# Layer 1's folded product moved into four PSUM banks, with sums and differences sharing a bank, and gate banks copied out under a raised priority

## The chip, the core and the metric

The kernel runs on one core of a Trainium2 chip. The metric is device time in microseconds (us) from start to end of one execution. TensorE (PE) multiplies and transposes, VectorE (DVE) and ScalarE (ACT) do elementwise work and read PSUM, GpSimd (POOL) and SyncE (SP) mostly issue DMAs. PSUM has eight banks of 512 fp32 columns; this kernel keeps them in two pools of four, named `pa` and `pm`.

## The reference

Two layers of a post-norm encoder over 512 tokens of width 2048, all in fp32. Per layer:

```python
mod = silu(c) @ w_ada[l] + b_ada[l];  shift, scale, gate = split(mod, 3)
h = layernorm(x) * (1 + scale) + shift
u_f, z_f, cq, ckv, k_r, z_a = split(h @ w_in[l], [1024, 2048, 2560, 2816, 2880])
# group A: 8 groups of 128 channels, 2-D FFT over tokens and channels, real part, a 128x128 map
y_f = einsum("sgc,gcd->sgd", real(fftn(u_f, axes=(s, c), norm="ortho")), w_fmix[l]) * silu(z_f)
# group B: latent attention, 8 heads, rotary key shared
y_a = attention(rmsnorm(cq) @ w_q_b, rmsnorm(ckv) @ w_kv_b, k_r) * silu(z_a)
x = layernorm(ALPHA * x + gate * (concat(y_f, y_a) @ w_out[l]), ln_g, ln_b)
```

## The kernel before, in words

Every fp32 product is made of three fp32r products: each operand is split into a high and a low part (`split`, lines 145 to 147: ACT casts the high part, line 146, then DVE subtracts, line 147), and `mm3` (lines 149 to 152) issues high·high, high·low and low·high. A weight unit is loaded by SP into a raw buffer `wr` (three of them), split by ACT and DVE, and then used by PE. The fp32 weights thus pass through ACT and DVE on their way to PE.

Layer 1 works on folded tokens: `h` holds sums of tokens t and t+256 in columns 0 to 255 and their differences in columns 256 to 511. Its input products run in this order: gate group ZA0 (`first_group`), gate group ZF0 (`fm_group`), the constants of the Fourier part (`folded_constants`), the folded Fourier product (`u_pass`), gate group ZF1 with the Fourier work in between (`fm_group` with `runner(fb, FW)`), then the latents CQ and CKV, and gate group ZA1. A gate group fills four `pa` banks; `unfolded` (lines 841 to 849) copies each bank out with ACT (line 845), forms sum and difference on DVE (lines 846, 847), applies SiLU on ACT (line 848) and stores to DRAM by SP (line 849).

`folded_constants` multiplies six 128x512 plain-fp32 products (line 554) into six `pm` banks, one after another in the four that there are. Each of the first kind is read in halves by ACT (line 561) and DVE (line 562), each of the second kind in four quarters by ACT (line 420) and DVE (line 421). The left operands are built by DVE copies (lines 550, 552).

`u_pass` takes 16 weight units from `fold_unit` (lines 390 to 408), each 1024 columns wide: 520 columns that go with the token sums (0 to 519) and 504 that go with the differences (520 to 1023). For each unit and each of two token halves p it issues three products: 264 columns into a `pa` bank, 256 columns into a `pm` bank, 504 columns into another `pa` bank. So it uses four `pa` and two `pm` banks. Afterwards the banks are split into `ue`, `un` and `uo`, and the row of token 0 (`xacc`, summed up on DVE) is multiplied by ones (lines 785, 786).

The order of instructions on each engine is set by a list scheduler when the program is built; at run time each engine goes through its list in that order, and waits by semaphores. `tc.high_priority(offset=...)` raises what is inside it in that scheduler. A bank from a pool is given again when its readers are done.

Of the kernel before, what the change touches and what calls it, by code (L numbers as in the profile page):

```python
# [18 lines left out]
P = 128  # L19
S = 512  # L20
D = 2048
NT = S // P
NK = D // P
# [59 lines left out]
def trunk_kernel(ctx: ExitStack, tc: tile.TileContext, x, c, positions, w_ada, b_ada, w_in, q_norm,  # L83
# [15 lines left out]
    ROWS, LR = [0, 2, 1, 3], 600  # L99

    FW, UAH = 2, 6


    XE, RN0, PL, WL = 8, 2, 1, 2
    V, A, GP, PE, SP = nc.vector, nc.scalar, nc.gpsimd, nc.tensor, nc.sync
# [14 lines left out]
    def nm(s):  # L120
        uid[0] += 1
        return f"{s}{uid[0]}"

    def big(shape, dt=F32R):
        return bp.tile(shape, dt, tag="b", name=nm("b"))
# [4 lines left out]
    def t2(shape, dt=F32):  # L130
        return t2p.tile(shape, dt, tag="t2", name=nm("t2"))
# [4 lines left out]
    def pa():  # L136
        return psa.tile([P, 512], F32, tag="pa", name=nm("pa"))

    def pm():
        return psm.tile([P, 512], F32, tag="pm", name=nm("pm"))  # L140

    def f(ap):
        return ap.bitcast(F32)

    def split(hi, lo, src):
        A.copy(hi, src)  # L146
        V.tensor_tensor(lo, src, f(hi), op=ALU.subtract)  # L147

    def mm3(o, lh, ll, rh, rl, first, last):
        PE.matmul(o, lh, rh, start=first, stop=False)  # L150
        PE.matmul(o, lh, rl, start=False, stop=False)  # L151
        PE.matmul(o, ll, rh, start=False, stop=last)  # L152
# [13 lines left out]
    for tb in range(NT):  # L166
        t = [big([P, 1024], F32) for _ in range(2)]
# [283 lines left out]
    st = Stream(4, 2)  # L451
# [167 lines left out]
    h = [None] * NK  # L619
# [34 lines left out]
    for l in range(DEPTH):  # L654
# [91 lines left out]
            return u  # L746


        def u_pass():

            e, o, b = [pa(), pa()], [pa(), pa()], [pm(), pm()]
            for k in range(NK):
                wh, wl = st.next()
                for p in range(2):
                    es, os_ = slice(p * P, p * P + P), slice(256 + p * P, 256 + p * P + P)
                    for bank, ts, cs in ((e[p], es, slice(256, 520)), (b[p], es, slice(0, 256)),
                                         (o[p], os_, slice(520, 1024))):
                        mm3(bank[:, :cs.stop - cs.start], h[k][:, 0, ts], h[k][:, 1, ts], wh[:, cs], wl[:, cs],
                            k == 0, k == NK - 1)
            un = big([P, 2, 2, 2, P])  # L760
            GP.memset(f(un), 0.0)
            ue, uo = [], []
            for p in range(2):
                t = big([P, 2, 512])
                split(t[:, 0, 256:512], t[:, 1, 256:512], e[p][:, 0:256])
                split(un[:, 0, p, 0, 120:128], un[:, 0, p, 1, 120:128], e[p][:, 256:264])
                ue.append(t)
            for p in range(2):
                t = big([P, 2, 8, 64])
                split(t[:, 0, :, 1:64], t[:, 1, :, 1:64], o[p][:, :504].rearrange("p (g c) -> p g c", c=63))  # L770
                for a in range(2):
                    V.memset(f(t[:, a, :, 0]), 0.0)
                uo.append(t.rearrange("p a g c -> p a (g c)"))
            for p in range(2):
                split(ue[p][:, 0, 0:256], ue[p][:, 1, 0:256], b[p][:, 0:256])

            onesr = t2([P, P], F32R)
            V.memset(f(onesr), 1.0)
            xa = big([P, 1024])
            xl = big([P, 1024])  # L780
            split(xa[:, :520], xl[:, :520], xacc[0][:, :520])
            xr = big([1, 2, 512])
            for c0, c1 in ((0, 256), (256, 520)):
                ps = pm()
                PE.matmul(ps[:, :c1 - c0], onesr, xa[:, c0:c1], start=True, stop=False)
                PE.matmul(ps[:, :c1 - c0], onesr, xl[:, c0:c1], start=False, stop=True)
                split(xr[0:1, 0, c0:c0 + 256], xr[0:1, 1, c0:c0 + 256], ps[0:1, 0:256])
                if c1 == 520:
                    split(un[0:1, 1, 0, 0, 120:128], un[0:1, 1, 0, 1, 120:128], ps[0:1, 256:264])
            return ue, uo, un, xr  # L790

        def fourier_folded(u):
            ue, uo, un, xr = u

            def cosines(dst, kk, rr, n):
                ps = pm()
                for k in range(2):
                    mm3(ps[:, 0:258], kk[k][0], kk[k][1], dt[k][:, 0, 0:258], dt[k][:, 1, 0:258], k == 0, False)
                for a in range(2):
                    PE.matmul(ps[:, 0:258], rr[a], odd, start=False, stop=a == 1)  # L800
                split(dst[:, 0, 0:n], dst[:, 1, 0:n], ps[:, 0:n])

            an = big([P, 2, S])
            cosines(an, [(un[:, 0, k, 0], un[:, 0, k, 1]) for k in range(2)], [un[0:1, 1, 0, a] for a in range(2)], 258)
            yield
            for b in range(4):
                bs = slice(b * P, b * P + P)
                at = big([P, 2, S])
                cosines(at, [(ue[k][:, 0, bs], ue[k][:, 1, bs]) for k in range(2)], [xr[0:1, a, bs] for a in range(2)], 257)
                ps = pm()  # L810
                for k in range(2):
                    mm3(ps[:, 0:256], uo[k][:, 0, bs], uo[k][:, 1, bs], dt[k][:, 0, 256:512], dt[k][:, 1, 256:512],
                        k == 0, k == 1)
                split(at[:, 0, 257:512], at[:, 1, 257:512], ps[:, 1:256])
                yield
                yf.append(big([P, 2, S], F32))
                for i in range(2):
                    g = 2 * b + i
                    y = yf[-1][:, i]
                    gs = slice((g % 4) * P, (g % 4) * P + P)  # L820
                    c, s_, n = cw[0][g // 4], cw[1][g // 4], nq[g // 4]
                    pp, pq = pm(), pm()
                    mm3(pp[:, 0:258], c[:, 0, gs], c[:, 1, gs], at[:, 0, 0:258], at[:, 1, 0:258], True, False)
                    mm3(pp[:, 0:258], n[:, 0, gs], n[:, 1, gs], an[:, 0, 0:258], an[:, 1, 0:258], False, True)
                    mm3(pq[:, 0:256], s_[:, 0, gs], s_[:, 1, gs], at[:, 0, 256:512], at[:, 1, 256:512], True, True)
                    ev = t2([P, 258])
                    A.copy(ev, pp[:, 0:258])
                    V.tensor_tensor(y[:, 1:256], ev[:, 1:256], pq[:, 1:256], op=ALU.subtract)
                    V.tensor_tensor(y[:, 257:512], ev[:, 1:256], pq[:, 1:256], op=ALU.add)
                    V.tensor_copy(y[:, 0:257:256], ev[:, 0:257:256])  # L830
                    yield
# [8 lines left out]

        def unfolded(banks, dst):

            for j in range(4):
                t, z = t2([P, S]), t2([P, S])
                A.copy(t, banks[j])
                V.tensor_tensor(z[:, 0:256], t[:, 0:256], t[:, 256:512], op=ALU.add)
                V.tensor_tensor(z[:, 256:512], t[:, 0:256], t[:, 256:512], op=ALU.subtract)
                A.activation(z, z, AF.Silu, scale=0.5)
                SP.dma_start(szd[dst + j], z)

        def runner(gen, n=1):
            def run():
                for _ in range(n):
                    next(gen, None)
            return run
# [229 lines left out]
        if l == 0:  # L1085

            for step, (k0, nk) in enumerate(STEPS):
# [44 lines left out]
                def pas():  # L1132
                    return [pa() for _ in range(NT)]

                def pieces(gen, then=iter(())):
                    def run():
                        next(then, None)
                        for _ in range(2):
                            next(gen, None)
                    return run  # L1140
# [6 lines left out]
                ub = k_group(UB, pas(), pieces(fa, lq))  # L1147
# [3 lines left out]
                fb = fourier(1, folded(ub))  # L1151
# [14 lines left out]
        else:  # L1166
            unfolded(first_group(), 0)
            st.ahead(4, UAH)
            with tc.issue_after(hold[0]):
                banks = fm_group(ada=G0)  # L1170
            unfolded(banks, H)
            cw, nq, dt = folded_constants(1)
            st.ahead(4, 2)
            fb = fourier_folded(u_pass())
            unfolded(fm_group(runner(fb, FW)), H + 4)
            drain(fb)
            gt = gates()
# [17 lines left out]
        es, pts = {}, {}  # L1195
        for i in range(len(todo) + WL):
# [9 lines left out]
            if i < 4:  # L1206
                for k in range(2 * i, 2 * i + 2):
                    t = big([P, 2, S])
# [36 lines left out]
        for g in range(4):  # L1245
            gs = slice(g * 512, (g + 1) * 512)
# [3 lines left out]
            if g < 3:  # L1250
                banks = [pa() for _ in range(NT)]
                for k2 in range(8):
                    tm_half(banks, st.next(), y, k2 * 2, 512, k2 == 0, k2 == 7)
                    if g == 0:
                        tb, j = k2 // 2, k2 % 2
# [11 lines left out]
            else:  # L1267
# [4 lines left out]
                banks = [pa() for _ in range(NT)]  # L1272
# [7 lines left out]
                for tb in ROWS if l == 0 else range(NT):  # L1280
                    ts = slice(tb * P, (tb + 1) * P)
                    for k in range(KO * 2, NK):
                        wh, wl = ws[k // 2 - KO]
# [68 lines left out]
```

## Time and profile before

| | |
|---|---|
| median of 3 runs | 1406.38 us (1401.28 to 1406.9) |
| the profiled execution | 1404.26 us, span 1402.5 us |
| PE busy | 1344.3 us, 96% of the span |
| DVE, ACT, POOL busy | 72%, 41%, 4% |
| mean granted TensorE clock | 0.990 |

Times in the trace are us from the start of the span. The rows further down give start, duration, engine, line and operation; output and inputs follow as tile names without numbers, then the shape; a bracket at the end tells how long the engine sat idle before and what ended that. Matmuls are pipelined, so their durations overlap: the distance between starts is what one costs.

### The profile page before, as it was taken

To read this page: it belongs to the slowest core of one execution; us is meant where nothing else is said; L and a number is where in the kernel's file an instruction comes from. 1 tells how busy PE (TensorE), PEld (TensorE's weight loads), DVE (VectorE), ACT (ScalarE), POOL (GpSimd) and SP (SyncE) were. 2 spreads that over 40 slices of the span, in tenths; PEclk is the share of its full clock that TensorE was granted. 3 is DMA by queue.
4 is the path that set the end of the run, shared out by engine and by line. 5 is a ranking of instruction groups with operands and counts; after the bars stand their busy time and mean duration, and the time that the engine had idled before them with its cause. 6 is when DMAs were issued, how large, how long until landed. Compare 5 with 4: busy or idle time off the path is not lost. (4 is left out here: it accounts for less than half of the span.)

```text
span 1402.5 us, 18691 instructions
## 1 busy us (share of the span) xinstructions
PE 1344.3 (96%) x6949; PEld 1141.2 (81%) x6949; DVE 1015.6 (72%) x1670; ACT 579.6 (41%) x1052; POOL 55.5 (4%) x82
## 2 busy tenths in 40 slices
PE   4899999999999999999988999998999999999996
PEld 3688888787888888788877888887898888888885
DVE  7899999849978986658588748567655576642448
ACT  6722332224437776112167524323234677721210
POOL 1000000000000000000030001011000000000001
PEclk9999999999999999999998999999999999999998
DMA  9988898824764444968336435369444221263323
GB/s 288 299 293 300 271 349 286 306 76 122 211 206 140 157 128 161 317 199 283 105 145 203 161 96 166 105 205 367 152 119 121 74 67 54 80 236 105 91 60 120
DMA packets 134546, 253.24 MB, mean 181 GB/s; under 512 B 19308, under 2 KB 50168, under 8 KB 134456
## 3 DMA queue, kind: packets, MB, share of 16 engines
q1 hardware_dynamic: 127416, 228.73, 50.1%
q0 software_dynamic: 7040, 23.34, 4.9%
q8 instruction: 54, 0.88, 0.3%
q14 instruction: 36, 0.29, 0.1%
HBM read 237.32 MB, written 14.70 MB: 180 GB/s over the span
## 5 line engine op out<-in xcount | busy, mean ns | idle before, releaser
L150 PE MATMUL pa<-b,b 128*128 128x512 f32 (+4 forms) x1432 | 537.4, 377 | 11.6 <-ACT b L146 5.5
L151 PE MATMUL pa<-b,b 128*128 128x512 f32 (+4 forms) x1432 | 535.9, 375 | 4.3 <-DVE ln_v L187 4.3
L152 PE MATMUL pa<-b,b 128*128 128x512 f32 (+4 forms) x1432 | 534.5, 374 | 1.9 <-DVE b L147 1.9
L146 ACT CAST b<-wr 128x1024 fp32r<-128x1024 f32 (+3 forms) x184 | 180.0, 988 | 356.1 <-PE pa L152 181.1
L150 PEld LDWEIGHTS pa<-b,b 128*128 128x128 f32 x1432 | 271.2, 190 | 59.7 <-ACT b L146 9.2
L151 PEld LDWEIGHTS pa<-b,b 128*128 128x128 f32 x1432 | 272.1, 190 | 48.1 <-DVE ln_v L187 4.6
L152 PEld LDWEIGHTS pa<-b,b 128*128 128x128 f32 x1432 | 271.5, 190 | 48.2 <-DVE b L147 2.9
L147 DVE TENSOR_TENSOR b<-wr,b 128x1024 fp32r<-128x1024 f32 (+3 forms) x184 | 208.1, 1141 | 136.5 <-PE pa L151 84.7
L246 DVE SCALAR_TENSOR_TENSOR acc<-ada,cact,acc 128x1024 f32<-128x1024 f32 (+2 forms) x193 | 227.2, 1184 | 23.1 <-DMA ada<-in_w_ada_dram 21.2
L150 PE MATMUL pm<-b,b 128*128 128x512 f32 (+3 forms) x594 | 201.7, 341 | 1.2 <-ACT b L146 0.8
L151 PE MATMUL pm<-b,b 128*128 128x512 f32 (+3 forms) x594 | 197.2, 333 | 0.0
L152 PE MATMUL pm<-b,b 128*128 128x512 f32 (+3 forms) x594 | 197.0, 333 | 0.0
L150 PEld LDWEIGHTS pm<-b,b 128*128 128x128 f32 x594 | 111.7, 189 | 17.8 <-ACT b L146 2.7
L151 PEld LDWEIGHTS pm<-b,b 128*128 128x128 f32 x594 | 112.3, 189 | 10.5
L152 PEld LDWEIGHTS pm<-b,b 128*128 128x128 f32 x594 | 112.2, 189 | 10.4
L146 ACT CAST b<-pm 128x512 fp32r<-128x512 f32 (+4 forms) x110 | 54.9, 530 | 72.6 <-PE pm L800 17.8
L147 DVE TENSOR_TENSOR b<-pm,b 128x512 fp32r<-128x512 f32 (+4 forms) x110 | 64.1, 610 | 23.6 <-ACT b L146 23.0
L1120 DVE TENSOR_TENSOR b<-b,pm 128x512 f32<-128x512 f32 (+1 forms) x88 | 55.5, 656 | 4.5 <-PE pm L152 4.1
L146 ACT CAST b<-t 128x512 fp32r<-128x512 f32 (+1 forms) x73 | 35.9, 525 | 31.4 <-PE pm L151 9.5
L1039 DVE TENSOR_REDUCE mx<-pa 128x1 f32<-128x512 f32 x64 | 42.9, 684 | 5.3 <-PE pa L1037 4.7
L1044 ACT ACTIVATE t<-t,ssum 128x512 f32<-128x512 f32 x64 | 45.9, 735 | 1.2 <-DVE ssum L1043 1.2
L1042 ACT ACTIVATE t<-pa,mx 128x512 f32<-128x512 f32 x64 | 44.0, 693 | 4.6 <-DVE mx L1039 4.5
(186 smaller groups left out, 1120.7 us busy)
## 6 DMA issues: line engine op xcount, KB each, us to landing
wr<-in_w_in_dram SPq DMA_DIRECT2D x105, 512.0 KB, 4.6
ada<-in_w_ada_dram SPq DMA_DIRECT2D x96, 512.0 KB, 5.3
wr<-in_w_out_dram SPq DMA_DIRECT2D x64, 512.0 KB, 4.1
ada<-in_w_ada_dram SPq DMA_DIRECT2D x96, 256.0 KB, 4.9
ada<-in_w_ada_dram POOLq DMA_DIRECT2D x32, 512.0 KB, 5.4
b<-in_x_dram SPq DMA_DIRECT2D x16, 512.0 KB, 6.3
ada<-in_w_ada_dram SPq DMA_DIRECT2D x32, 192.0 KB, 5.3
wr<-in_w_q_b_dram SPq DMA_DIRECT2D x48, 128.0 KB, 3.0
```

Source lines behind the costliest of these rows:

```text
L146: A.copy(hi, src)
L147: V.tensor_tensor(lo, src, f(hi), op=ALU.subtract)
L150: PE.matmul(o, lh, rh, start=first, stop=False)
L151: PE.matmul(o, lh, rl, start=False, stop=False)
L152: PE.matmul(o, ll, rh, start=False, stop=last)
L246: V.scalar_tensor_tensor(out=a, in0=t[:, r - r0], scalar=cact[:, r:r + 1], in1=a, op0=ALU.mult, op1=ALU.add)
L1039: V.reduce_max(mx, ps, axis=AX.X, negate=True)
L1042: A.activation(e, ps, AF.Exp, bias=mx, accum_out=ssum)
L1044: A.activation(e, e, AF.Copy, scale=ssum)
L1120: V.tensor_tensor(s_[tb], s_[tb], banks[tb][:, :n], op=ALU.add)
```

## The change

Only layer 1 is touched. `u_pass` becomes `u_start`, `u_step` and `u_finish`. All of the folded product now lies in four `pm` banks, two for each token half p. Each bank holds 260 of the 520 sum columns in its columns 0 to 259 and 252 of the 504 difference columns in its columns 260 to 511, so that each unit and half has four products (260, 260, 252, 252 columns) in place of three. Only the first product in a bank has the start flag. The split after it reads each bank in two or three pieces. The columns of zeros in `uo` are set by POOL and no longer by DVE. `unfolded` copies all four banks first, under `tc.high_priority(offset=300)`, and needs four temporaries up front.

```diff
+    EV = 300
-        def u_pass():
-            e, o, b = [pa(), pa()], [pa(), pa()], [pm(), pm()]
-            for k in range(NK):
-                wh, wl = st.next()
-                for p in range(2):
-                    es, os_ = slice(p * P, p * P + P), slice(256 + p * P, 256 + p * P + P)
-                    for bank, ts, cs in ((e[p], es, slice(256, 520)), (b[p], es, slice(0, 256)),
-                                         (o[p], os_, slice(520, 1024))):
-                        mm3(bank[:, :cs.stop - cs.start], h[k][:, 0, ts], h[k][:, 1, ts], wh[:, cs], wl[:, cs],
-                            k == 0, k == NK - 1)
+        def u_start():
+            return [[pm(), pm()] for _ in range(2)]
+        def u_step(banks, k):
+            wh, wl = st.next()
+            hk = h[k]
+            for p in range(2):
+                for x in range(2):
+                    ts = slice(256 * x + p * P, 256 * x + p * P + P)
+                    n = 252 if x else 260
+                    for b in range(2):
+                        cs = slice(520 * x + b * n, 520 * x + b * n + n)
+                        mm3(banks[p][b][:, 260 * x:260 * x + n], hk[:, 0, ts], hk[:, 1, ts], wh[:, cs], wl[:, cs],
+                            k == 0 and x == 0, k == NK - 1 and x == 1)
+        def u_finish(banks):
...
+                a, b = banks[p]
                 t = big([P, 2, 512])
-                split(t[:, 0, 256:512], t[:, 1, 256:512], e[p][:, 0:256])
+                split(t[:, 0, 0:260], t[:, 1, 0:260], a[:, 0:260])
+                split(t[:, 0, 260:512], t[:, 1, 260:512], b[:, 0:252])
+                split(un[:, 0, p, 0, 120:128], un[:, 0, p, 1, 120:128], b[:, 252:260])
...
+                for i, ps in enumerate((a, b)):
+                    gs = slice(4 * i, 4 * i + 4)
+                    split(t[:, 0, gs, 1:64], t[:, 1, gs, 1:64], ps[:, 260:512].rearrange("p (g c) -> p g c", c=63))
+                for x in range(2):
+                    GP.memset(f(t[:, x, :, 0]), 0.0)
...
         def unfolded(banks, dst):
+            ts = [t2([P, S]) for _ in range(4)]
+            with tc.high_priority(offset=EV):
+                for j in range(4):
+                    A.copy(ts[j], banks[j])
             for j in range(4):
-                t, z = t2([P, S]), t2([P, S])
-                A.copy(t, banks[j])
+                t, z = ts[j], t2([P, S])
```

The order of instructions changes at a few places. Line numbers of the changed kernel are 2 higher up to `u_pass` and 10 to 16 higher behind it: 152 to 154 are `mm3`, 148 and 149 `split`, 556 the products of the constants, 423 their quarters on DVE, 856 the copies of `unfolded`. Numbers in names tell tiles apart.

Place 1 is the start of the folded product, where the constants are made. On PE before, four of the six products of the constants are followed by folded products into `pa` banks; the last two come in between:

```order
L554 MATMUL pm_7851<-b_7811,b_7848 128x512
L150 MATMUL pa_7889<-b_7552,b_6732 128x264
L151 MATMUL pa_7889<-b_7553,b_6732 128x264
L152 MATMUL pa_7889<-b_7552,b_6732 128x264
L150 MATMUL pa_7891<-b_7552,b_6732 128x504
L554 MATMUL pm_7862<-b_7811,b_7859 128x512
L554 MATMUL pm_7872<-b_7811,b_7870 128x512
```

On PE now, the six stand together and the folded product behind them; its fourth bank, `pm_7892`, is entered after two products of the second unit:

```order
L154 MATMUL pm_7891<-b_7552,b_6732 128x252
L152 MATMUL pm_7889<-b_7592,b_6735 128x260
L153 MATMUL pm_7889<-b_7593,b_6735 128x260
L152 MATMUL pm_7892<-b_7552,b_6732 128x260
L153 MATMUL pm_7892<-b_7553,b_6732 128x260
L154 MATMUL pm_7892<-b_7552,b_6732 128x260
```

What moved: before, the first product into a `pm` bank of the folded product stands behind 19 of its products into `pa` banks; now all of them go to `pm`, the pool that the constants use.

At the same place on DVE now, where `pm_7872` is the bank of the last constant (`fc_7874` its result), and `b_7993`, `wr_7941` belong to a weight unit:

```order
L400 TENSOR_TENSOR b_7993<-wr_7941 128x504
L423 SCALAR_TENSOR_TENSOR fc_7874<-pm_7872,ident,fc_7874 128x128
L410 SCALAR_TENSOR_TENSOR xacc_7560<-b_7993,orow,xacc_7560 128x520
L149 TENSOR_TENSOR b_7995<-b_7993,b_7994 128x1024
L423 SCALAR_TENSOR_TENSOR fc_7874<-pm_7872,ident,fc_7874 128x128
```

The last read of `pm_7872` stands behind the subtraction of a whole weight unit there, as it did before. Further up on DVE the copies that build left operands of the constants (line 550 before) now stand ahead of the sums and differences of all four gate banks:

```order
L552 COPY b_7848<-b_7809 128x64 x2
L552 COPY b_7859<-b_7809 128x64
L859 TENSOR_TENSOR t_7789<-t_7781 128x256
L860 TENSOR_TENSOR t_7789<-t_7781 128x256
L859 TENSOR_TENSOR t_7794<-t_7782 128x256
```

Before, the sums and differences of three banks came first:

```order
L552 COPY b_7835<-b_7809 128x128
L846 TENSOR_TENSOR t_7782<-t_7781 128x256
L847 TENSOR_TENSOR t_7782<-t_7781 128x256
L846 TENSOR_TENSOR t_7789<-t_7788 128x256
L847 TENSOR_TENSOR t_7789<-t_7788 128x256
L846 TENSOR_TENSOR t_7796<-t_7795 128x256
L847 TENSOR_TENSOR t_7796<-t_7795 128x256
L550 COPY b_7848<-b_7809 128x64 x2
L550 COPY b_7859<-b_7809 128x64 x2
```

Place 2 is the end of the folded product, on ACT. Before, the reads of the six banks alternate between banks; the cast of `xacc` comes after eight of them:

```order
L146 CAST b_8321<-pa_7889 128x256
L146 CAST b_8321<-pm_7893 128x256
L146 CAST b_8319<-pa_7889 128x8
L146 CAST b_8326<-pa_7890 128x256
L146 CAST b_8331<-pa_7891 128x8x63
L146 CAST b_8326<-pm_7894 128x256
L146 CAST b_8319<-pa_7890 128x8
L146 CAST b_8336<-pa_7892 128x8x63
L146 CAST b_8347<-xacc_7560 128x520
```

Now two or three reads of one bank follow each other; DVE has the same order:

```order
L148 CAST b_8415<-pm_7889 128x260
L148 CAST b_8422<-pm_7889 128x4x63
L148 CAST b_8415<-pm_7890 128x252
L148 CAST b_8413<-pm_7890 128x8
L148 CAST b_8422<-pm_7890 128x4x63
L148 CAST b_8429<-pm_7891 128x260
L148 CAST b_8436<-pm_7891 128x4x63
L148 CAST b_8445<-xacc_7560 128x520
```

On PE the product that takes the cast of `xacc` (line 785, now 795) stood six products behind the folded product, and stands three behind it now.

Place 3 is ACT after gate group ZF1, where `pa_8364` to `pa_8367` before (`pa_8462` to `pa_8465` now) are its banks and `wr_8872`, `wr_8905` before (`wr_8970`, `wr_9003` now) are weight units of CQ. Before:

```order
L845 COPY t_8836<-pa_8364 128x512
L845 COPY t_8843<-pa_8365 128x512
L848 ACTIVATE t_8837<-t_8837 128x512
L146 CAST b_8934<-wr_8872 128x1024
L848 ACTIVATE t_8844<-t_8844 128x512
L845 COPY t_8850<-pa_8366 128x512
L146 CAST b_8967<-wr_8905 128x1024
L845 COPY t_8857<-pa_8367 128x512
```

And now:

```order
L856 COPY t_8934<-pa_8462 128x512
L148 CAST b_9032<-wr_8970 128x1024
L856 COPY t_8935<-pa_8463 128x512
L856 COPY t_8936<-pa_8464 128x512
L148 CAST b_9065<-wr_9003 128x1024
L856 COPY t_8937<-pa_8465 128x512
```

The SiLUs moved behind the copies; the two weight casts stay among the copies, the first of them one copy earlier. After ZF0 and ZA1 the four copies now stand together; after ZA0 one weight cast stays before the fourth.

## Rows read from the trace of the kernel before

**Rows 1.** stretches: length, busy PE, PEld, DVE, ACT, POOL, granted clock, DMA, GB/s

```profile
840.00:891.00 51.00, 51.00 (x306) 43.95 (x305) 42.40 (x79) 24.36 (x60) 4.90 (x7) 1.00 0.55 160
891.00:949.00 58.00, 58.00 (x313) 49.32 (x312) 32.87 (x54) 15.38 (x30) 7.92 (x15) 1.00 0.51 161
949.00:963.00 14.00, 10.25 (x37) 7.24 (x36) 8.94 (x17) 6.90 (x11) 1.58 (x3) 0.84 1.04 405
```

**Rows 2.** groups of PE by form: count, busy us, mean ns; plain-fp32 products

```profile
L554 PE MATMUL pm<-b,b 128*128 128x512 f32 x12 | 5.5, 599 | 0.0
```

**Rows 3.** timeline of PE: start, duration, what; a long run and seven units

```profile
835.75 0.39 PE L150 MATMUL pa<-b,b 128*128 128x512 f32 x1
839.60 0.39 PE L152 MATMUL pa<-b,b 128*128 128x512 f32 x1
852.16 0.28 PE L150 MATMUL pa<-b,b 128*128 128x264 f32 x1
871.69 0.29 PE L150 MATMUL pa<-b,b 128*128 128x264 f32 x1
```

**Rows 4.** timeline of PE where the constants are made

```profile
839.83 3.59 PE L554 MATMUL pm<-b,b 128*128 128x512 f32 x8
843.91 1.96 PE L554 MATMUL pm<-b,b 128*128 128x512 f32 x4
848.36 0.34 PE L150 MATMUL pm<-b,b 128*128 128x256 f32 x1
```

**Rows 5.** timelines of DVE and ACT at that place

```profile
834.36 0.30 DVE L550 COPY b<-b 128x64 f32<-128x64 f32 x2 [4.92 <-PE pa L151]
839.97 0.49 DVE L550 COPY b<-b 128x64 f32<-128x64 f32 x4
...
841.56 0.42 DVE L847 TENSOR_TENSOR t<-t 128x256 f32<-128x256 f32 x1
841.89 0.74 DVE L562 TENSOR_TENSOR fc<-pm,fc 64x256 fp32r<-64x256 f32 x2
...
850.75 0.37 ACT L420 ACTIVATE fc<-pm,ident 128x128 fp32r<-128x128 f32 x1 [1.19 <-DVE fc L421]
...
850.37 0.35 DVE L421 SCALAR_TENSOR_TENSOR fc<-pm,ident,fc 128x128 fp32r<-128x128 f32 x1
852.48 1.23 DVE L147 TENSOR_TENSOR b<-b,b 128x1024 fp32r<-128x1024 f32 x1 [0.23 <-ACT b L146]
853.62 0.34 DVE L421 SCALAR_TENSOR_TENSOR fc<-pm,ident,fc 128x128 fp32r<-128x128 f32 x1
```

**Rows 6.** timelines of ACT, DVE and PE where the folded product ends

```profile
887.60 0.37 ACT L146 CAST b<-pa 128x256 fp32r<-128x256 f32 x1 [4.15 <-PE pa L152]
888.01 0.42 DVE L147 TENSOR_TENSOR b<-pa,b 128x256 fp32r<-128x256 f32 x1 [2.93 <-ACT b L146]
...
888.52 0.17 ACT L146 CAST b<-pa 128x8 fp32r<-128x8 f32 x1 [0.20 <-DVE b L147]
890.53 0.67 ACT L146 CAST b<-xacc 128x520 fp32r<-128x520 f32 x1
...
889.84 0.40 PE L150 MATMUL pa<-b,b 128*128 128x512 f32 x1
891.26 0.51 PE L785 MATMUL pm<-b,t 128*128 128x256 f32 x2
```

**Rows 7.** timelines of ACT and PE after gate group ZF1

```profile
952.68 1.07 ACT L845 COPY t<-pa 128x512 f32<-128x512 f32 x2
957.19 1.04 ACT L146 CAST b<-wr 128x1024 fp32r<-128x1024 f32 x1 [2.47 <-DMA ada<-in_w_ada_dram]
...
959.29 0.80 PE L150 MATMUL pa<-b,b 128*128 128x512 f32 x1 [2.94 <-ACT t L845]
```

**Rows 8.** the same columns in short stretches

```profile
760.00:764.00 4.00, 3.42 (x16) 2.88 (x15) 3.17 (x8) 4.00 (x10) 0.00 (x0) 0.57 0.26 56
...
960.00:962.00 2.00, 2.00 (x6) 1.21 (x4) 1.36 (x2) 1.20 (x2) 0.35 (x1) 0.50 1.05 408
```

More of the change, by code (lines that the diff above doesn't have):

```diff
@@ L763, in u_pass @@
             for p in range(2):
+                a, b = banks[p]
                 t = big([P, 2, 512])
-                split(t[:, 0, 256:512], t[:, 1, 256:512], e[p][:, 0:256])
-                split(un[:, 0, p, 0, 120:128], un[:, 0, p, 1, 120:128], e[p][:, 256:264])
+                split(t[:, 0, 0:260], t[:, 1, 0:260], a[:, 0:260])
+                split(t[:, 0, 260:512], t[:, 1, 260:512], b[:, 0:252])
+                split(un[:, 0, p, 0, 120:128], un[:, 0, p, 1, 120:128], b[:, 252:260])
                 ue.append(t)
-            for p in range(2):
                 t = big([P, 2, 8, 64])
-                split(t[:, 0, :, 1:64], t[:, 1, :, 1:64], o[p][:, :504].rearrange("p (g c) -> p g c", c=63))
-                for a in range(2):
-                    V.memset(f(t[:, a, :, 0]), 0.0)
+                for i, ps in enumerate((a, b)):
[3 more added lines that the diff above has]
+                    GP.memset(f(t[:, x, :, 0]), 0.0)
                 uo.append(t.rearrange("p a g c -> p a (g c)"))
-            for p in range(2):
-                split(ue[p][:, 0, 0:256], ue[p][:, 1, 0:256], b[p][:, 0:256])
             onesr = t2([P, P], F32R)
@@ L1173, in trunk_kernel @@
             st.ahead(4, 2)
-            fb = fourier_folded(u_pass())
+            ub = u_start()
+            for k in range(NK):
+                u_step(ub, k)
+            fb = fourier_folded(u_finish(ub))
             unfolded(fm_group(runner(fb, FW)), H + 4)
```

## The prediction

> **What bounds the kernel now.** I began with the busy time by stretch. Through the folded product and gate group ZF1 PE is busy all of the 51.00 and all of the 58.00 us at a granted clock of 1.00 [rows 1]; the reader is to see that there is no idle time there for a change to win, only some to lose. After ZF1 PE is busy 10.25 of 14.00 us, so 3.75 us are idle, and DMA moves 405 GB/s; this is the one place in reach of the change with something to gain. Next I read the timelines of PE, DVE and ACT around the three places, with the brackets that tell what ended an idle time, and at last the granted clock in short stretches. PE is the bound, so a term counts where it makes PE wait or gives it more to do; DVE and ACT count only through the banks that they free.
>
> **More and narrower products.** Each unit now has 24 matmuls instead of 18, the columns equal (6144), so 96 more in 16 units. A long run of 512-column products starts every (839.60 - 835.75)/17 = 0.2265 us [rows 3]; a unit of 18 products takes (871.69 - 852.16)/7 = 2.79 us [rows 3]. Solved together (0.2265 = 512a + f; 2.79 = 6144a + 18f) they give some 0.012 us fixed per product, so 96 x 0.012 = +1.15 us. The lower end is 0 (the two differences are small against the rounding of the rows). The upper end rests on something that the trace doesn't have: a product of this kind with under 256 columns. 192 of the products are now 252 wide. The nearest dearer row is plain fp32: the four L554 products last 3.59 us in eight records of 0.599 [rows 2, 4], so a record starts every (3.59 - 0.60)/7 = 0.427 us and a product costs 0.854, or 0.42 for 252 columns, against 0.118 by the line above: 192 x 0.303 = +58 us. I take +1.15, since the products of 256 and 264 columns in the 2.79 us follow the same line as those of 512.
>
> **The start of the folded product.** Before, PE goes from 839.83 through the six constants to its first product in a `pm` bank at 848.36 with no idle bracket [rows 4]: the products into `pa` cover the reads of the constants' banks. This cover is gone. On DVE, a copy that builds a constant's operand was held 4.92 us by a product of ZF0, and the later ones ran at 839.97 [rows 5]; they now stand ahead of all eight sums and differences, which so start at about 840.3. Each takes 841.89 - 841.56 = 0.33 to 0.34 [rows 5], and they end at 843.0. Then come two halves of banks (0.37 each, from 0.74 for two [rows 5]), 0.4 of copies and a memset (an estimate from 0.49 for four copies), and the second half of the first bank: free at 844.5. PE is done with the first four constants at 839.83 + 4 x 0.854 = 843.25 and waits 1.3 for this bank. The fifth and sixth take 1.7, to 846.25. The folded product's first bank is that of the third constant, read in four quarters by ACT (0.37) and DVE (0.35) [rows 5]; behind three halves and four quarters, with the 0.20 that a handover cost at 888.52 [rows 6], it is free at about 847.6: idle 1.3. Twenty small products (2.4 us) go to 850.0, and there PE needs the bank of the last constant. Its last quarter stands on DVE behind the subtraction of a whole weight unit (1.23), as before, when it ran 853.62 to 853.96 and nobody asked for it [rows 5]. Before, it was 853.96 - 850.37 = 3.6 behind the second quarter; now the second comes at about 848.8 (after a half, a quarter and a 504-column sum of 0.6, estimated as 504/1024 of 1.23), so the bank is free at 852.4: idle 2.5. Behind PE's waiting product stands all the rest of the folded product, hence the three waits count in full: **+5.1 us**. Lower end +2.6, if the copies are not held by PE and the sums end as early as before, or the last read slips in ahead of the subtraction; upper end +6.6, if ACT's SiLUs, now between the casts of these banks, delay each handover.
>
> **The end of the folded product.** `xacc`'s cast took 0.67 from 890.53, and PE's product on it at 891.26 came 1.42 after the folded product's end at 889.84, with no idle time [rows 6]. Now only three products of 0.23 stand in between, so PE is there 0.7 after the end. On ACT the cast comes after seven pieces. ACT and DVE take turns in a bank: the 8-column cast waited 0.20 for DVE's subtraction from another part of the same bank [rows 6], and the constants' quarter 1.19 [rows 5]. Two or three pieces of one bank now stand one behind the other, so the chain is, piece by piece where they don't overlap, 3 x (0.37 + 0.42) + 0.42 + 0.37 + 2 x 0.17 + 0.42 + 0.37 + 0.67 = 4.9 [rows 6]; it starts when the first half's banks are complete, some 1.6 before the end, and leads to 3.2 after it. PE waits **+2.5 us**. Lower end +0.25 (casts that need not wait for DVE run through in 3 us), upper +3.2.
>
> The Trainium skill, "PSUM — Partial Sum Buffer", section "PSUM bank collisions raise a hardware error", says that two engines must not be in the same bank and quadrant at once even at different columns, and that one guards by bank. By it the pieces of a bank can't overlap and the sum has 2.5 here; without it, 0.25. The 0.20 at 888.52 agrees with it, between columns that don't overlap.
>
> **After ZF1.** Before, two banks were copied from 952.68 in 1.07, then a cast waited for its weights until 957.19 and took 1.04, and PE sat idle 2.94 until 959.29 for the next copy [rows 7]. Now the cast stands behind the first copy, so the second bank comes only after 957.19 + 1.04 + 0.53 = 958.76, and PE has only the six products (1.4) of the first bank for the meantime: about 4.1 idle. The second bank's six products, done before the wait until now, come behind it: the third bank's begin at 958.76 + 1.36 = 960.1 and not at 959.29, so the net is **+0.8**. Queued behind the waiting cast on ACT are two copies, and behind them PE's products into their banks. Upper end +2 (those six at the 0.50 of 960 to 962 [rows 8]); lower end -6.0: should the weights land before the copies are due, the 3.75 idle and what the clock takes there, 14.00 x (1 - 0.84) = 2.2 [rows 1], vanish.
>
> **The clock.** Where PE idled shortly, 760 to 764 shows 3.42 busy of 4.00 and a granted clock of 0.57 [rows 8], the 2.4 GHz level partly fallen to 1.2: 4 x 0.43 = 1.7 us lost. One such fall for the two new places with waits: **+1.7**, between 0 (none falls) and 4.4 (both fall, by the 2.2 of the stretch after ZF1).
>
> Costing nothing: four memsets that go from DVE to POOL, busy 4.90 of 51 us [rows 1]; copies grouped after ZF0, ZA0 and ZA1, since PE shows no wait on them there (after ZF1 it does); the later start of weight units on DVE, busy 42.4 of 51 us [rows 1], since PE starts later by more.
>
> **The sum.** 1.15 + 5.1 + 2.5 + 0.8 + 1.7 = +11.25. The profiled execution took 1404.26, 2.1 under the median of 1406.38: 1415.5 by the one, 1417.6 by the other. I say 1416.
>
> **The rivals.** (1) Not slower: raising the copies sets banks free sooner after ZF1. The bound is the DMA of the weights. If the cast's unit has landed when its turn comes, the term is -6.0 in place of +0.8, and with the waits at the lower ends (2.6, 0.25) and no fall of the clock the time is 1404.26 + 1.15 + 2.85 - 6.0 = 1402.3; with the waits as forecast, 1404.26 + 8.75 - 6.0 = 1407.0. For it: 3.75 us idle there. Against: 405 GB/s in that stretch, and the cast waited for a DMA, not for ACT. It turns the sign from a landing about 4 us earlier. (2) The 252-column products cost as plain fp32: 1404.26 + 11.25 + 58 = 1474. For it: no row shows a narrower one than 256. Against: the same operands, dtype and flags. (3) The clock falls at both waits, by as much as after ZF1: 4.4 in place of 1.7, 1420 by the median. For it: the half clock that follows the wait there. Against: the new idle times are shorter, 1.3 to 2.5 where that one was 2.94.
>
> **How the numbers follow.** The forecast 0.55 (its own range 1411 to 1420), rival 1 0.21, rival 2 0.12, rival 3 0.12. A difference under 0.5%, 7.0 us, can't be told from none. Faster, below 1399.4, needs rival 1 with every wait at its lowest and something more: 0.05. Within 0.5%, up to 1413.4: the other 0.16 of rival 1 and 0.08 of the forecast, 0.24. Slower: 0.71. The range 1403 to 1426 leaves out rival 2 and the ends of the others.
>
> **What would show it.** Right: PE idle before the fifth constant, the first `pm` product and the fourth bank (in all 4 to 6 us), the last two ended by DVE's quarters; 2 to 3 us before the product on `xacc`, ended by ACT; 24 products in 2.85 us per unit. Wrong: these places without idle brackets (the theory of banks falls), a unit near 6.5 us (rival 2), or weights landed before ACT's copies after ZF1 (rival 1).

## The result, and the profile after

The changed kernel took 1417.28 us (median of 4 runs, 1415.6 to 1418.63) against 1406.59 before (4 runs): ratio 1.0084, 95% interval 1.0058 to 1.0111, so 10.7 us slower. The forecast was 1416. Its profiled execution took 1417.05 us, with a span of 1415.2, that is 12.7 more than the span of before.

The timeline of PE, at the places that the prediction speaks of (the first constant; the fifth; the first product in a `pm` bank; the fourth `pm` bank; the first product of gate group ZF1; the product on `xacc`; the two banks waited for after ZF1; and the first transposes of the latents, far behind):

```profile
843.42 3.59 PE L556 MATMUL pm<-b,b 128*128 128x512 f32 x8
848.88 1.96 PE L556 MATMUL pm<-b,b 128*128 128x512 f32 x4 [1.86 <-DVE fc L564]
851.95 0.36 PE L152 MATMUL pm<-b,b 128*128 128x260 f32 x1 [1.12 <-DVE fc L564]
857.40 0.36 PE L152 MATMUL pm<-b,b 128*128 128x260 f32 x1 [2.84 <-DVE fc L423]
862.18 0.28 PE L152 MATMUL pm<-b,b 128*128 128x260 f32 x1
881.96 0.28 PE L152 MATMUL pm<-b,b 128*128 128x260 f32 x1
900.34 0.39 PE L152 MATMUL pa<-b,b 128*128 128x512 f32 x1
903.42 0.51 PE L795 MATMUL pm<-b,t 128*128 128x256 f32 x2 [2.22 <-ACT b L148]
967.38 0.50 PE L152 MATMUL pa<-b,b 128*128 128x512 f32 x1 [0.29 <-ACT t L856]
972.20 0.69 PE L152 MATMUL pa<-b,b 128*128 128x512 f32 x1 [3.17 <-ACT t L856]
1021.86 2.17 PE L911 MATMUL pm<-ident,b 128*128 128x128 f32 x16 [0.86 <-DVE b L905]
```

The end of ZF1 and the same last mark before, in the timeline of PE:

```profile
953.31 0.50 PE L150 MATMUL pa<-b,b 128*128 128x512 f32 x1 [0.64 <-ACT t L845]
1009.12 2.17 PE L898 MATMUL pm<-ident,b 128*128 128x128 f32 x16 [0.86 <-DVE b L892]
```

Three cuts tell where the 12.7 us are. Up to the first constant the kernel is 843.42 - 839.83 = 3.6 later [rows 4]; the second profile of each kernel (below), where both begin it at 842.1, shows that this is scatter of the start. From the first constant to the end of the folded product it took 900.34 - 843.42 = 56.92 against 889.84 - 839.83 = 50.01 [rows 4, 6]: **+6.91**. From there to the transposes it took 121.52 against 1009.12 - 889.84 = 119.28: **+2.24**. Behind the transposes both take the same. So the change costs 9.15 in this pair of executions.

Of the 6.91, the brackets at 848.88, 851.95 and 857.40 make up 1.86 + 1.12 + 2.84 = 5.82; before, no product there waited. Seven units of 24 products take 881.96 - 862.18 = 19.78 against 19.53 for seven of 18 [rows 3], or 0.036 more per unit and 0.57 in 16. The remaining 0.52 comes from how a bracket counts: it begins at the recorded end of the product before, which lies 0.16 behind the time at which the next one would have started (0.28 long, one every 0.12; 0.17 with the constants), three times some 0.5. From start to start the three stops cost 6.4. DVE and POOL in the first wait, DVE in the third, by their timelines:

```profile
843.39 0.42 DVE L552 COPY b<-b 128x64 f32<-128x64 f32 x3 [4.99 <-PE pa L153]
847.08 0.99 DVE L552 COPY b<-b 128x64 f32<-128x64 f32 x1
847.18 0.95 DVE L554 COPY b<-b 128x128 f32<-128x128 f32 x1
855.76 1.22 DVE L149 TENSOR_TENSOR b<-b,b 128x1024 fp32r<-128x1024 f32 x1 [0.23 <-ACT b L148]
856.91 0.34 DVE L423 SCALAR_TENSOR_TENSOR fc<-pm,ident,fc 128x128 fp32r<-128x128 f32 x1
```

```profile
846.15 1.86 POOL L559 MEMSET fc<- 128x1024 f32 x2
```

The sums and differences stand behind the operand copies of 843.39, as forecast, and end before 847; two further copies then took 0.99 and 0.95 (overlapping, 1.05 together), beside two memsets on POOL, the second of which ended at 848.01. In the third wait the last quarter (856.91) stands behind the subtraction of a whole weight unit (855.76), and PE goes on 0.15 after it ends.

At the end of the folded product, and after ZF1, the timeline of ACT:

```profile
899.65 0.64 ACT L148 CAST b<-pm 128x252 fp32r<-128x252 f32 x2 [0.50 <-DVE b L149]
900.89 0.17 ACT L148 CAST b<-pm 128x8 fp32r<-128x8 f32 x1 [0.60 <-DVE b L149]
902.74 0.63 ACT L148 CAST b<-xacc 128x520 fp32r<-128x520 f32 x1
965.79 1.05 ACT L148 CAST b<-wr 128x1024 fp32r<-128x1024 f32 x1 [4.11 <-DMA wr<-in_w_in_dram]
970.62 1.04 ACT L148 CAST b<-wr 128x1024 fp32r<-128x1024 f32 x1 [3.30 <-DMA ada<-in_w_ada_dram]
```

A piece of a bank from which another piece has just been read waits for DVE's read of that other piece (0.50, 0.60), the cast of `xacc` ends at 903.37, and PE's product on it begins at 903.42 after 2.22 idle. After ZF1 the cast that stands between the first and the second copy runs 970.62 to 971.66, once its weights are there. Busy time and granted clock (columns as in [rows 1]) in the stretch behind the `xacc` product and in 28 us that begin some 4 us ahead of the end of ZF1, and then in the like 28 us before:

```profile
904.00:908.00 4.00, 4.00 (x13) 3.19 (x12) 2.79 (x8) 1.94 (x6) 0.00 (x0) 0.57 0.00 0
963.00:991.00 28.00, 24.54 (x101) 19.50 (x100) 19.88 (x28) 10.18 (x15) 3.21 (x7) 0.94 1.01 374
```

```profile
949.00:977.00 28.00, 24.25 (x93) 18.76 (x92) 20.16 (x30) 10.75 (x15) 3.17 (x6) 0.88 1.03 388
```

Behind the 2.22 us wait PE is busy throughout but at 0.57: 4 x 0.43 = 1.7 lost. After ZF1 it idles 28 - 24.54 = 3.5 against 3.75, and the clock takes 28 x 0.06 = 1.7 against 28 x 0.12 = 3.4. So 2.22 + 1.7 - 0.3 - 1.7 = 1.9 of the 2.24.

### The profile page after: what moved, and what is told of

The parts are those of the page before. It is cut to its first block, busy times and chain, and to the rows that moved or that the text cites. A ratio compares the mean times of both kernels' runs of the same rounds, so it can differ in the third digit from the quotient of the medians.

```text
span 1415.2 us, 18904 instructions
## 1 busy us (share of the span) xinstructions
PE 1347.9 (95%) x7045; PEld 1146.2 (81%) x7045; DVE 1017.9 (72%) x1668; ACT 579.6 (41%) x1054; POOL 55.8 (4%) x86
## 5 line engine op out<-in xcount | busy, mean ns | idle before, releaser
L152 PE MATMUL pa<-b,b 128*128 128x512 f32 (+2 forms) x1368 | 515.6, 379 | 10.8 <-ACT b L148 5.5
L153 PE MATMUL pa<-b,b 128*128 128x512 f32 (+2 forms) x1368 | 514.5, 377 | 4.3 <-DVE ln_v L189 4.3
L154 PE MATMUL pa<-b,b 128*128 128x512 f32 (+2 forms) x1368 | 513.4, 376 | 1.9 <-DVE b L149 1.9
L152 PEld LDWEIGHTS pa<-b,b 128*128 128x128 f32 x1368 | 259.5, 191 | 57.0 <-ACT b L148 8.8
L154 PEld LDWEIGHTS pa<-b,b 128*128 128x128 f32 x1368 | 260.2, 190 | 47.4 <-DVE b L149 3.2
L153 PEld LDWEIGHTS pa<-b,b 128*128 128x128 f32 x1368 | 260.2, 190 | 46.9 <-DVE ln_v L189 4.6
L152 PE MATMUL pm<-b,b 128*128 128x512 f32 (+5 forms) x690 | 228.5, 333 | 5.5 <-DVE fc L423 2.8
L153 PE MATMUL pm<-b,b 128*128 128x512 f32 (+5 forms) x690 | 223.9, 325 | 0.0
L154 PE MATMUL pm<-b,b 128*128 128x512 f32 (+5 forms) x690 | 223.4, 325 | 0.0
L152 PEld LDWEIGHTS pm<-b,b 128*128 128x128 f32 x690 | 129.6, 188 | 23.2 <-issue 5.6
L153 PEld LDWEIGHTS pm<-b,b 128*128 128x128 f32 x690 | 130.2, 189 | 10.6
L154 PEld LDWEIGHTS pm<-b,b 128*128 128x128 f32 x690 | 130.0, 189 | 10.5
L148 ACT CAST b<-pm 128x512 fp32r<-128x512 f32 (+5 forms) x118 | 57.1, 516 | 82.3 <-PE pm L810 20.0
L149 DVE TENSOR_TENSOR b<-pm,b 128x512 fp32r<-128x512 f32 (+5 forms) x118 | 66.7, 592 | 32.3 <-ACT b L148 31.5
```

## The experiments

"The stretch" is the time on PE from the first constant to the first transposes of the latents: 169.29 before, 178.44 after the change. Ratios are to the kernel before in the same session (11 to 19 executions of it, median 1404.8 to 1405.7).

### The folded product alone, the copies alone

`u_only` is the changed kernel with the old `unfolded`, `ev_only` the kernel before with the new one. The edit of the first, which the second makes the other way round:

```diff
-            ts = [t2([P, S]) for _ in range(4)]
-            with tc.high_priority(offset=EV):
-                for j in range(4):
-                    A.copy(ts[j], banks[j])
             for j in range(4):
-                t, z = ts[j], t2([P, S])
+                t, z = t2([P, S]), t2([P, S])
+                A.copy(t, banks[j])
```

> Only the folded product in four pm banks; the copies of the gate groups as before. Theory of banks: waits at the start of the folded product of 4 to 5 us (the first one shorter than 1.86, since the sums and differences are not all behind the operand copies), 2.2 us and a half clock at its end, 1.1 us for the products, after gate group ZF1 the 3.7 us of before: 8 to 10 us slower than before, 1415 to 1417. Rival, the raised copies are the cause: within 3 us of before, 1406 to 1409.

> Only the raised copies; the folded product in six banks as before. Theory of banks: no waits at the start and the end of the folded product, -1.7 to +1 after ZF1: 1404 to 1408, no difference that can be told. Rival, the raised copies are the cause: 1413 or more.

Measured: `u_only` 1416.4 us, ratio 1.0081 (1.0065 to 1.0096); `ev_only` 1404.54, ratio 1.0000 (0.9989 to 1.0011). The loss lies in the folded product; the copies alone change nothing that can be told. PE in `u_only` at its start, and busy time and clock there:

```profile
847.72 1.95 PE L556 MATMUL pm<-b,b 128*128 128x512 f32 x4 [0.50 <-DVE fc L564]
852.14 0.36 PE L152 MATMUL pm<-b,b 128*128 128x260 f32 x1 [2.47 <-DVE fc L564]
857.90 0.56 PE L152 MATMUL pm<-b,b 128*128 128x260 f32 x1 [1.56 <-DVE fc L423]
```

```profile
856.00:860.00 4.00, 2.44 (x12) 2.17 (x12) 3.38 (x6) 1.42 (x5) 0.00 (x0) 0.50 0.52 136
860.00:864.00 4.00, 4.00 (x20) 4.00 (x20) 3.18 (x4) 1.28 (x4) 0.00 (x0) 0.50 0.43 132
```

The first wait is down from 1.86 to 0.50, since without the raised copies not all sums stand behind the operand copies; the second is up, and the three add to 4.53 as expected. The operand copies also run clear of POOL's memset there (they end at 844.91, the memset begins at 846.81). But here the clock fell too, to 0.50 for a whole 8 us, and it did not fall behind the 2.23 us wait at the end of the folded product, where a half clock was expected: 904 to 912 shows 1.00. In `ev_only` a wait of 0.69 stands before the fifth constant, where none was expected: the raised copies alone put the sums behind the operand copies. After ZF1 PE waits as before (0.46 and 3.02 for 0.64 and 2.94), since a weight cast still stands among the copies:

```profile
961.00 0.79 PE L152 MATMUL pa<-b,b 128*128 128x512 f32 x1 [3.02 <-ACT t L848]
```

### The constants in the other pool

`const_pa` takes `pa` banks for all six products of the constants, `last_pa` for the sixth alone:

```diff
-                ps = pm()
+                ps = pa()
```

```diff
-                ps = pm()
+                ps = pa() if hf and a == 2 else pm()
```

> The changed kernel with the six products of the constants in pa banks, which the folded product no longer uses. Theory of banks: the first pm products no longer wait for readers, the 5.8 us at the start fall to 0 to 1.5 (a wait for the first pa bank before the fifth constant may stay): 4.3 to 5.8 us less than the changed kernel, about 1412. Rival, 96 more and narrower products are the cause: the waits are hidden elsewhere and 1417 stays.

> The changed kernel with only the last constant's product in a pa bank; the other five stay in pm banks. Theory of banks: the 2.84 us wait before the fourth pm bank of the folded product goes or falls below 1, since no folded product needs that bank, and the 1.86 before the fifth constant stays: some 2.5 us less from the first constant to the end of the folded product (56.9 before), 1414 to 1416. Rival, the handover between ACT and DVE or DVE's work at that place is the bound: another pm bank is as late and a wait of 2 us or more stays.

Measured: `const_pa` 1409.5 us, ratio 1.0034 (1.0019 to 1.0048); `last_pa` 1410.76, ratio 1.0044 (1.0026 to 1.0061). PE in each, with every bracket that there is from the first constant to the end of the folded product, then the longer wait after ZF1 in `const_pa`:

```profile
849.04 1.96 PE L556 MATMUL pa<-b,b 128*128 128x512 f32 x4 [1.03 <-DVE fc L564]
...
968.10 0.79 PE L152 MATMUL pa<-b,b 128*128 128x512 f32 x1 [3.43 <-ACT t L856]
```

```profile
845.67 1.10 PE L556 MATMUL pa<-b,b 128*128 128x512 f32 x2 [1.26 <-DVE t L788]
849.41 0.36 PE L152 MATMUL pm<-b,b 128*128 128x260 f32 x1 [0.60 <-DVE fc L564]
```

With `const_pa` 1.03 of the 5.82 stay, and from the first constant to the end of the folded product it is 51.64 in place of 56.92: the products of constants that hold `pm` banks are the cause. With `last_pa` the third wait is gone altogether, as expected, and it is 52.71, 4.2 less where 2.5 was expected. The 1.86 did not stay: the last constant, in its `pa` bank, now goes ahead of the fifth, and the wait of 1.26 is before it. In `const_pa` 2 us of the 5.3 are lost again behind the folded product (123.51 where the changed kernel took 121.52): 0.6 as idle time after ZF1 (0.64 + 3.43 for 0.29 + 3.17), the rest at the lower clock. This execution was the slowest of the eight (1413.92 us, median 1409.5), and the changed kernel's own two profiles have 3.46 and 5.30 of idle time there; so whether anything is lost again for the sake of the edit isn't shown.

### The reads of the constants raised

```diff
+                        with tc.high_priority(offset=EV): scaled(...)
```

The reads in halves (lines 563 and 564) are raised in the same way.

> The changed kernel with the reads of the constants' banks raised, so that DVE reads the last quarter ahead of the weight unit. Theory: the 2.84 us wait before the fourth pm bank falls below 1 and the 1.86 before the fifth constant shrinks as well: 2 to 4 us less than the changed kernel, 1413 to 1415. Rival, the handover between ACT and DVE is the bound and not the order on DVE: within 1 us of the changed kernel.

Measured: 1415.62 us, ratio 1.0072 (1.0056 to 1.0087), and 57.04 from the first constant to the end of the folded product. DVE at the third wait, and PE:

```profile
857.21 1.23 DVE L149 TENSOR_TENSOR b<-b,b 128x1024 fp32r<-128x1024 f32 x1 [0.23 <-ACT b L148]
858.35 0.35 DVE L423 SCALAR_TENSOR_TENSOR fc<-pm,ident,fc 128x128 fp32r<-128x128 f32 x1
```

```profile
858.84 0.36 PE L152 MATMUL pm<-b,b 128*128 128x260 f32 x1 [2.55 <-DVE fc L423]
```

The miss is one of the edit: the raised reads came earlier at the front, but the last quarter stands behind the weight unit as before. And the operand copies now stand behind the raised reads, so that the first wait, ended by such a copy (line 552), is 1.97; with the 2.55 the brackets make up 4.52 in place of 5.82. The 1.3 went to the clock, 0.66 from 849 to 854: 5 x 0.34 = 1.7. What the last quarter would bring ahead of the weight unit isn't shown by this run; `last_pa` shows what it brings when no folded product needs its bank.

### The two copies beside POOL's memset

```diff
-                        V.tensor_copy(lhs[:, d * 64:d * 64 + 64], cc[:, a, 0:64])
+                        (A.copy if hf and a else V.tensor_copy)(lhs[:, d * 64:d * 64 + 64], cc[:, a, 0:64])
...
```

The copy in line 554 is given to ACT in the same way, for the last constant.

> The changed kernel in which ACT and not DVE copies the last two operands of the constants, which stood on DVE beside a memset of POOL and took 0.99 and 0.95 us in place of some 0.2. Theory: the two copies are held by POOL's memset; without them on DVE the 1.86 us wait before the fifth constant falls by 0.7 to 0.9, to about 1.0, and the memset lasts 1.86 as before. Rival, DVE's order alone sets that wait: it falls by the 0.2 to 0.3 that undisturbed copies take, to 1.6.

```profile
845.69 1.95 PE L556 MATMUL pm<-b,b 128*128 128x512 f32 x4 [1.13 <-DVE fc L564]
```

One execution, 1415.07 us beside 1400.46 of the kernel before: the first wait is 1.13, 0.73 less. The first theory holds for the size, but two things changed in this run: POOL's memsets, 1.86 for the two as before, ran already at 827.98. Other runs settle it: in `reads_first`, where they also ran early (831.28), the same two copies on DVE took 0.18 and 0.21, and in all nine runs in which they stand beside the memsets 0.95 to 1.00.

### The products on xacc later

The cast stands first in `u_finish`, and the loop with the products moves into the first step of `fourier_folded`:

```diff
         def u_finish(banks):
...
+            split(xa[:, :520], xl[:, :520], xacc[0][:, :520])
             ue, uo = [], []
...
-            split(xa[:, :520], xl[:, :520], xacc[0][:, :520])
...
-            for c0, c1 in ((0, 256), (256, 520)):
...
         def fourier_folded(u):
...
+            for c0, c1 in ((0, 256), (256, 520)):
```

> The changed kernel with the cast of xacc ahead of the reads of the banks, and the four products on it behind the first unit of gate group ZF1. Theory: the 2.22 us wait at the end of the folded product and the half clock behind it (about 1.7 us) go: 3 to 4 us less than the changed kernel, 1413 to 1414. Rival, PE is held by the bank that the products go into and not by the cast: a wait of 1.5 us or more stays there, 1416 to 1417.

Measured: 1413.76 us, ratio 1.0065 (1.0051 to 1.0079). The 2.22 us wait is gone and the clock behind it stays at 1.00, so 118.09 in place of 121.52 from the end of the folded product on: 3.4 less, as expected (2.7 by the ratios). But in this execution, the slowest of five (1415.99), the clock fell at the start of the folded product, where the changed kernel's first profile shows 1.00 (58.46 in place of 56.92):

```profile
856.00:860.00 4.00, 1.70 (x9) 1.73 (x10) 3.77 (x6) 1.67 (x5) 0.00 (x0) 0.83 0.47 133
902.00:906.00 4.00, 4.00 (x23) 3.42 (x22) 2.16 (x7) 2.53 (x7) 0.00 (x0) 1.00 0.00 0
```

### The copies ahead of the casts after ZF1

The two casts that stood among the copies (`held[2:]`) are tied to come behind the last copy (the two units ahead of them are cast before the copies):

```diff
+            with tc.issue_after(last): [st.units[st.pos + j].conv() for j in held[2:]]
```

> The changed kernel, in which the two weight casts that stand among the four copies after gate group ZF1 come behind all four. Theory: the 3.17 us wait before the second bank and the half clock behind it (1.6 us) go, and a wait of 0 to 1.5 us for the next weight unit comes in their place: 3 to 5 us less than the changed kernel, 1412 to 1414. Rival, the weights' DMA is the bound there and PE waits for the weight unit instead: no difference, 1416 to 1418.

Measured: 1412.14 us, ratio 1.0046 (1.0029 to 1.0063), the stretch 174.06, 4.4 less than the changed kernel. One short wait is left there, and the granted clock behind it is 1.00:

```profile
967.74 0.50 PE L152 MATMUL pa<-b,b 128*128 128x512 f32 x1 [0.90 <-ACT t L854]
```

```profile
967.00:971.00 4.00, 3.26 (x14) 2.70 (x15) 3.67 (x4) 2.81 (x6) 0.53 (x1) 1.00 1.04 407
```

### All three together, and the old folded product with the copies ahead

`best` has the edits of `const_pa`, `xacc_late` and `copies_first`; `six_first` is `ev_only`, with the old `u_pass`, and the edit of `copies_first`. In both:

```diff
-            unfolded(fm_group(runner(fb, FW)), H + 4)
+            unfolded(fm_group(runner(fb, FW)), H + 4, (2, 3, 4, 5))
```

> The changed kernel with the constants in pa banks, the late products on xacc, and the copies ahead of the casts. If the three places are independent their gains add up: 5 + 3.5 + 4 = 12.5 us less than the changed kernel, 1403 to 1406, 1 to 3 us below the kernel before. If what one place gives is lost at the next (the weights' DMA is the bound): 1409 or more.

> The folded product in six banks as before, the copies raised, and after gate group ZF1 the casts behind all four copies. If the gain of the best version comes from the copies alone and the four banks give nothing: 3 to 5 us less than before, 1401 to 1403, like the best version or 1 us under it. If the four banks are part of the gain (pa banks free for the next gate group): 1405 or more.

Measured: `best` 1402.9 us, ratio 0.9984 (0.9972 to 0.9995), 0.2% under the kernel before with an interval that is just clear of 1, and by the two ratios 1.0% under the changed one; `six_first` 1400.97, ratio 0.9977 (0.9967 to 0.9987). Their stretches are 164.01 and 163.15. The 28 us around the end of ZF1, which cost 3.75 of idle time and 3.4 of clock before, are in `best` without either, and in `six_first` the same but for 0.07 idle:

```profile
952.00:980.00 28.00, 28.00 (x125) 23.05 (x124) 21.62 (x30) 10.04 (x14) 3.98 (x8) 1.00 1.03 385
```

The gain over before comes from the copies ahead of the casts. The four banks show none of their own: the intervals overlap, and the stretch is 0.86 longer with them, near the 0.57 for 96 more products. In either a wait stays before the fifth constant (1.03 and 0.69).

### Both kernels once more

> The kernel before once more, for its profile. In the two profiles at hand the first product of the constants begins at 839.83 before and at 843.42 after the change, ahead of all that was changed. If this 3.6 us is scatter of the start, it begins between 840 and 845 here and the stretch from there to the first transpose of the latents stays at 169.3; if it belongs to the change, it begins at 839.8 again.

> The changed kernel once more, for its profile. The stretch from the first product of the constants to the first transpose of the latents was 178.4; if the granted clock falls in another place than at the end of the folded product, as with only the folded product changed, the stretch differs by 1 to 3 us while the idle times stay at 1.86, 1.12, 2.84 and 2.22.

```profile
842.13 3.59 PE L554 MATMUL pm<-b,b 128*128 128x512 f32 x8
892.15 0.40 PE L150 MATMUL pa<-b,b 128*128 128x512 f32 x1
1010.16 2.17 PE L898 MATMUL pm<-ident,b 128*128 128x128 f32 x16 [0.87 <-DVE b L892]
```

```profile
842.12 3.59 PE L556 MATMUL pm<-b,b 128*128 128x512 f32 x8
847.57 1.95 PE L556 MATMUL pm<-b,b 128*128 128x512 f32 x4 [1.86 <-DVE fc L564]
850.65 0.36 PE L152 MATMUL pm<-b,b 128*128 128x260 f32 x1 [1.12 <-DVE fc L564]
856.10 0.56 PE L152 MATMUL pm<-b,b 128*128 128x260 f32 x1 [2.84 <-DVE fc L423]
900.49 0.39 PE L152 MATMUL pa<-b,b 128*128 128x512 f32 x1
903.57 0.76 PE L795 MATMUL pm<-b,t 128*128 128x256 f32 x2 [2.22 <-ACT b L148]
974.14 0.79 PE L152 MATMUL pa<-b,b 128*128 128x512 f32 x1 [4.53 <-ACT t L856]
1024.35 2.17 PE L911 MATMUL pm<-ident,b 128*128 128x128 f32 x16 [0.86 <-DVE b L905]
...
856.00:860.00 4.00, 3.90 (x21) 3.94 (x22) 3.50 (x5) 1.26 (x3) 0.00 (x0) 0.59 0.43 136
904.00:908.00 4.00, 4.00 (x14) 3.29 (x14) 2.31 (x6) 1.94 (x6) 0.00 (x0) 0.62 0.00 0
```

The first of these stretches in the first profile of the changed kernel:

```profile
856.00:860.00 4.00, 2.60 (x22) 2.63 (x23) 3.50 (x6) 1.46 (x5) 0.00 (x0) 1.00 0.45 131
```

The first constant begins at 842.13 and 842.12: the 3.6 us of the first pair are scatter. The old folded product takes 50.02 again, and the stretch 168.03. The changed one shows 1.86, 1.12, 2.84 and 2.22 to the hundredth, but the clock fell at 856 too (4 x 0.41 = 1.6), and the waits after ZF1 were 0.77 and 4.53: the stretch was 182.23. So the change costs 9.2 to 14.2 by these four profiles, and the median of the runs, 10.7, lies between.

## Why the prediction was right, step by step

The likeliest case came in: 1417.28 for 1416, and the waits stand where it put them.

- **Start of the folded product**, +5.1 forecast, 5.82 measured by the brackets (1.3, 1.3, 2.5 against 1.86, 1.12, 2.84), 6.4 from start to start. The first was short by the two copies beside POOL's memset, priced at their undisturbed length (0.73 less without them there, in `lhs_act`). The cause, constants that hold the pool's banks, is shown by `const_pa` and `last_pa`.
- **End of the folded product**, +2.5 forecast, 2.22 measured, ended by the cast as said; `xacc_late` takes it away. The rule of the Trainium skill, "PSUM — Partial Sum Buffer", section "PSUM bank collisions raise a hardware error", held: by it one guards by bank, so that the pieces of one bank take turns, and ACT's waited 0.50 and 0.60 for DVE's.
- **More products**, +1.15 forecast, 0.57 measured: the step that failed in size. Two rows that differ by little gave 0.012 us per product; the units give 0.57/96 = 0.006. A unit takes 19.78/7 = 2.83 and not the 6.5 of rival 2, which is out.
- **After ZF1**, +0.8 forecast, -1.7 to -2 measured in the first pair, some +2 in the second (123.86 - 118.01 = 5.85 from the folded product's end to the transposes, less the 2.22 and 1.5 of clock behind it). The prediction took the weights to land as late against PE as before, and PE to idle 4.1. Before, the cast began 4.5 behind the end of ZF1 (957.19 [rows 7] against 953.31 - 0.64), and after the change 3.5 (970.62 against 967.38 - 0.29); in the second profiles it was 4.2 and 5.4. The seven profiles that have the new folded product and this order after ZF1 idle 3.5 to 5.3 there, 4.1 in the mean; the two of the kernel before 3.75 and 3.9. So the idle time that was forecast holds in the mean, and its effect in one pair is mostly scatter. Rival 1 asked for a landing 4 us sooner; the most seen was 1.
- **The clock**, +1.7 forecast, 1.7 measured in the first profile, where it fell behind the 2.22 us wait and not at the start; in the second it fell at both (1.6 + 1.5 = 3.1), which is rival 3 in kind, for its 4.4. Which of the places it takes differs from run to run.

By the first pair of profiles the sum was 9.15 for 11.25: the place after ZF1 gave 2.8 less and the start 0.7 to 1.3 more. By the second it was 14.2. That the median of the runs, 10.7, lies within a us of the forecast is in part luck: the start was priced too low and the products too high, and the place after ZF1 and the clock scatter by several us from run to run.

## What to carry to other kernels

When a long product moves into a pool, ask who else holds that pool's banks at its start and who needs them at its end: six short products before it cost 5.8 us here, though a unit of products took only 0.04 longer. A copy that frees a bank for PE must not stand behind a cast that waits for a transfer; putting four copies ahead of two casts was worth 3 us with the old folded product (`six_first`) and some 5 with the new one (`copies_first`), while the rearrangement itself cost 10.7. And a small wait of PE is dear by the half clock behind it, which may double it in one run and not in the next.

## What the hardware showed unasked

- DVE's copies from SBUF to SBUF took 0.99 and 0.95 us while POOL's memset ran, and 0.42 for three elsewhere in the same timeline; DVE's reads of PSUM right before (0.74 for two) were not stretched. The Trainium skill, "SBUF — State Buffer", section "Who interferes with whom", says that DVE copies in a mode with two ports and POOL's instructions take one shared pair of ports, and that the second waits until the first is done. The copy's end at 848.07, 0.06 behind the memset's, agrees, and so do the 0.18 and 0.21 of the same two copies in `reads_first`, where no memset of POOL ran beside them.
- Three idle times of 1.86, 1.12 and 2.84 us within 11 us left the clock at 1.00 over the next 4 us in one execution of the changed kernel; in another the same three, to the hundredth, were followed by 0.59.
